# A hybrid encoder on one core: two norms' sums taken through TensorE in reduced-precision halves, and half of a late token tile scaled by GpSimd and VectorE

## The chip, the core and the metric

The program runs on one core of a Trainium2 chip. The core has a matrix engine (TensorE, PE in the profile, whose weight loads are listed apart as PEld), three engines for elementwise work (VectorE or DVE, ScalarE or ACT, GpSimd or POOL), and SyncE (SP), which here only issues transfers. Every engine runs its own queue of instructions in order; they wait for one another through semaphores. Matrix products are accumulated in PSUM, and everything else lies in SBUF. The metric is the device time of one execution in microseconds (us), the median of several runs.

## What is computed

The input is a sequence of 512 tokens with 1024 features, in float32. It passes two layers, each a mixer and an MLP with a residual sum, and a last norm:

```python
for layer in range(DEPTH):                       # DEPTH = 2
    h = rms_norm(x, norm_mix[layer])
    y = stick_breaking_attention(h, ...) if layer % 2 == 0 else rglru_block(h, ...)
    x = x + y
    h = rms_norm(x, norm_mlp[layer])
    x = x + squared_relu_mlp(h, mlp_w1[layer], mlp_w2[layer])
return rms_norm(x, norm_final)

def rms_norm(x, g):
    return x * lax.rsqrt(jnp.mean(x * x, axis=-1, keepdims=True) + EPS) * g
```

The change bears on three of the five norms: the one ahead of the attention, the one ahead of the second mixer (a gated linear recurrence behind a convolution of four taps), and the last one.

## The kernel before

**Layout.** Up to the last MLP the residual stream is held with features on the partitions: 8 tiles `x[c]` of 128 features by 512 tokens. There the mean of squares of a token runs across partitions, and TensorE takes it: a matmul with a 128x128 tile of ones as weights adds up the partitions and leaves the sum on all 128 of them. At the very end tokens are on the partitions: four token tiles `t` of 128 tokens, each in two halves `h` of 512 features, `y(t, h)`. There a norm is a sum along the row.

**Precision.** Almost all products are made in three reduced-precision matmuls (type fp32r): a float32 operand `a` is rounded to a high half (a copy into an fp32r tile, on ScalarE), and the low half is what is left (a subtraction, on VectorE); `high x high`, `high x low` and `low x high` are added up in PSUM. A matmul whose operands are plain float32 is issued by the chip as two pieces, each with a weight load of its own. The two norms of the change are made with such plain float32 matmuls: `ones` and the moving operand are float32 tiles.

**Norm 1** (`inverse`, lines 452 to 484, ahead of the attention). The first products run on the unnormed input, and the inverse root mean square comes later. Eight tiny matmuls put the sum of squares of each token on its partition (`pc`, 128x4); ScalarE takes the root and VectorE the reciprocal `rc`. To have the same numbers along the free axis, VectorE scales the identity by each column of `rc`, four instructions of 128x128 into the tile `diag` (line 473), and TensorE multiplies it by `ones` (line 479): the result `pr` holds the inverse of each token on all partitions. ScalarE copies it to `r` (line 482). The copies `rp` and `rn` with the factors of the scores are made just behind `diag`. These VectorE instructions have high priority for the planner (below). What waits for `r` are the scores' scaling (line 593) and the key halves (line 373).

**Norm 2** (`norm`, `rms`, `inverse` of the second mixer, lines 1580 to 1592). `sq.acc` collects the squares of 8 feature tiles, the last four by VectorE (line 162). In the midst of the product of slab `c2` (a slab is 1024x128 of the input weights) TensorE multiplies `sq.acc` by `ones` (line 1582), ScalarE takes the root (step `N`), VectorE the reciprocal (step `r`).

**The order around it.** TensorE's order is written by hand throughout. In the second mixer ScalarE and VectorE too follow an order written by hand, the string `ORDER`: each step is a letter and a slab, for instance `fz0` fetches the raw weights of slab z0, `az0` rounds them (ScalarE), `xz0` makes their low half (VectorE), `jc3` does so by a transfer that accumulates, `Pz0` multiplies, `n0` scales by `r`, `b0` and `t0` apply the taps, `h0` and `l0` split the result, `G0` multiplies it by the gates' weights. Each instruction of these steps goes behind the one of the step before on its engine (class `Ordered`; its instructions stand under line 789 in the profile). The beginning reads

```python
R0 fz0 fz1 fc3 Pc2 fc4 az0 xz0 az1 N W2 r Pz0 fc5 ac3 jc3 W0 n0 xz1 b0 ac4 t0 fz2 Pz1 W1 jc4 n1 h0 X1
```

Raw weights rotate through three buffers and one more: a fetch on SP's queue waits until the slab that had the buffer has been rounded and subtracted. Elsewhere a planner orders ScalarE, VectorE, GpSimd and SP by a simulation of the program; `tc.issue_after(...)` only holds an instruction behind another of its engine.

**The tail** (`end`, lines 1792 to 1850). The last products of the second MLP arrive one by one and `collect` adds each to `y(t, h)` on VectorE (line 789 in the profile; `mlp.gained` is the last of them). The half h = 0 of the token tiles 2 and 3 comes last, tile 3 in two parts of 256 columns. Helpers: `square` sums the squares of a half (ScalarE, line 1745), `root` takes root (ScalarE, 1764) and reciprocal (VectorE, 1765), `scaled` multiplies a half by the weights `gb` of the last norm (GpSimd, in written order), `one` multiplies a half that is so scaled by the inverse (ScalarE 1787, or VectorE 1789), `both` does both in one instruction (VectorE, 1778), and both of these store the result (SP, 1769). So a half is finished either by `scaled` and `one` or by `both`. `scaled(..., behind=...)` makes GpSimd read a column of another half first, and so wait until that half is done.

Of the kernel before, what the change touches and what calls it, by code (L numbers as in the profile page):

```python
# [11 lines left out]
F32 = mybir.dt.float32  # L12
# [36 lines left out]


ORDER = """
R0 fz0 fz1 fc3 Pc2 fc4 az0 xz0 az1 N W2 r Pz0 fc5 ac3 jc3 W0 n0 xz1 b0 ac4 t0 fz2 Pz1 W1 jc4 n1 h0 X1
ac5 n2 fc6 X0 b2 l0 b1 X2 jc5 G0 t1 az2 Pc3 t2 s0 fz3 h1 ac6 z1 l1 h2 W3 l2 jz2 m0 G1 z0 fc7 n3 G2 s1 X3
R4 Pc4 b3 m1 T0 t3 s2 xc6 E0 E1 fz4 T1 fz6 h3 Pc5 az3 n4 d0 b4 jz3 m2 ac7 t4 E2 T2 jc7 d1 Pz2 n5 q0 d2
h4 az4 l3 W4 k0 fz5 q1 az6 G3 q2 z2 W5 X4 Pc6 b5 k1 fz7 g0 l4 g2 xz4 jz6 t5 g1 fo0 G4 s3 n6 Pz3 y1 h5 y0
# [9 lines left out]
def hybrid_encoder(  # L65
# [41 lines left out]
    def f(ap):  # L107
        return ap.bitcast(F32)
# [7 lines left out]

    dense_ones = work.tile([P, S], BF16, tag="sq", name="dense_ones")
    V.memset(dense_ones[:, :P], 1.0)
    ones = const.tile([P, P], F32, tag="ones", name="ones")
    V.memset(ones, 1.0)  # L120
    ident = const.tile([P, P], F32, tag="ident", name="ident")
    make_identity(nc, ident)
    eps_t = small.tile([P, 16], F32, tag="eps", name="eps_t")[:, :1]
    V.memset(eps_t, EPS)

    xgh = const.tile([P, C, S], F32R, tag="xgh", name="xgh")
# [178 lines left out]
    with ExitStack() as actx:  # L305
# [148 lines left out]
        def inverse():  # L454

            pc = bank("z")
            for t in range(NB):
                PE.matmul(
                    pc[:, t : t + 1], sums[:, t * P : (t + 1) * P], ones[:, 0:1],
                    start=True, stop=True,  # L460
                )
            rc, rp, rn = (small.tile([P, NB], F32, tag=n, name=n) for n in ("rc", "rp", "rn"))
            diag = work.tile([P, S], F32, tag="sq", name="diag")
            with tc.high_priority():
                norm["root"] = A.activation(rc, pc[:, :NB], AF.Sqrt, bias=eps_t, scale=1.0 / D)
                V.reciprocal(rc, rc)
                with tc.issue_after(norm["root"].ins):
                    A.activation(
                        small.tile([P, 1], F32, tag="rt", name="early", bufs=2), eps_t, AF.Sigmoid
                    )  # L470
                for t in range(NB):
                    ts = slice(t * P, (t + 1) * P)
                    V.tensor_scalar(diag[:, ts], ident, rc[:, t : t + 1], None, ALU.mult)
                V.tensor_scalar(rp, rc, SCALE, None, ALU.mult)
                V.tensor_scalar(rn, rc, -SCALE, None, ALU.mult)
            norm.update(rc=rc, rp=rp, rn=rn)
            yield
            pr = bank("z")
            PE.matmul(pr, ones, diag, start=True, stop=True)
            r = work.tile([P, S], F32, tag="r", name="r")  # L480
            with tc.high_priority():
                norm["copy"] = A.copy(r, pr)
            norm["r"] = r
            yield
# [1016 lines left out]
    with ExitStack() as rctx:  # L1501
# [77 lines left out]

        def norm():  # L1580
            ps["norm"] = bank("z")
            PE.matmul(ps["norm"], ones, sq.acc, start=True, stop=True)

        def rms():
            nonlocal r
# [91 lines left out]
        def out_low(c):  # L1677
# [1 line left out]

        STEPS = {  # L1680
            "f": fetch, "a": weights_high, "x": weights_low, "j": weights_added, "P": product,
            "N": rms, "r": inverse, "R": gate_raw, "W": gate_high, "X": gate_low, "G": gates,
            "n": scaled, "b": first_tap, "t": taps, "h": high, "l": low, "s": sigmoids,
            "m": gated_input, "T": tanh, "E": exp, "d": decay, "q": root, "k": recur,
            "z": gate, "g": gelu, "y": times_gate, "u": out_high, "i": out_low,
# [22 lines left out]
    with ExitStack() as mctx:  # L1708
        lp = mctx.enter_context(tc.tile_pool(name="last", bufs=1))
        mlp = Mlp(mctx, 1)  # L1710

        def transposed(h):

            mlp.turns = count(8 * h + 2 * (1 - h))
            for t in range(NB):
                pt = mlp.bank()
                for i in range(4):
                    PE.transpose(
                        pt[:, i * P : (i + 1) * P], x[4 * h + i][:, t * P : (t + 1) * P], ident
                    )  # L1720
                A.copy(mlp.y(t, h), pt)
                mlp.begun.add((t // 2 * 2 + h, t % 2))
            mlp.turns = count(4)

        gb = []
        EG = Ordered(G)

        def factors():
            for h in range(2):
                gb.append(home_tile(*HOMES[h], "gb"))  # L1730
                nc.sync.dma_start(
                    out=gb[h], in_=g_final[:, h * S : (h + 1) * S].broadcast_to([P, S])
                )


        A.activation(lp.tile([P, 1], F32, tag="rt", name="early"), eps_t, AF.Sqrt)

        ss = lp.tile([P, 40], F32, tag="ss", name="ss")[:, : 3 * NB]
        ss = ss.rearrange("p (t i) -> p t i", t=NB)
        bias = lp.tile([P, NB], F32, tag="bias", name="bias")  # L1740

        def square(t, h, i, cols=slice(0, S), end=False):

            junk = work.tile([P, S], F32, tag="sq", name="junk")
            A.activation(
                junk[:, cols], mlp.y(t, h)[:, cols], AF.Square, accum_out=ss[:, t, i : i + 1]
            )
            if not end:
                return A.activation(
                    bias[:, t : t + 1], ss[:, t, i : i + 1], AF.Identity,  # L1750
                    bias=bias[:, t : t + 1] if i else eps_t, scale=1.0 / D,
                )

        def scaled(t, h, cols=slice(0, S), behind=None):

            if behind is not None:
                seen = lp.tile([P, 1], F32, tag="seen", name="seen")
                EG.tensor_copy(seen, behind[:, :1])
            y = mlp.y(t, h)[:, cols]
            EG.tensor_tensor(y, y, gb[h][:, cols], ALU.mult)  # L1760

        def root(t, i):
            rt = small.tile([P, 1], F32, tag="rt", name="rt", bufs=2)
            A.activation(rt, ss[:, t, i : i + 1], AF.Sqrt, bias=bias[:, t : t + 1], scale=1.0 / D)
            V.reciprocal(rt, rt)
            return rt

        def store(t, h, cols=slice(0, S)):
            nc.sync.dma_start(
                out=out[t * P : (t + 1) * P, h * S + cols.start : h * S + cols.stop],  # L1770
                in_=mlp.y(t, h)[:, cols],
            )

        def both(t, h, rt, cols=slice(0, S), last=None):

            y = mlp.y(t, h)[:, cols]
            with tc.issue_after(last.ins) if last else nullcontext():
                done = V.scalar_tensor_tensor(y, y, rt, gb[h][:, cols], ALU.mult, ALU.mult)
            store(t, h, cols)
            return done  # L1780

        def one(t, h, rt, cols=slice(0, S), e=A, last=None):

            y = mlp.y(t, h)[:, cols]
            if e is A:
                with tc.issue_after(last.ins) if last else nullcontext():
                    A.activation(y, y, AF.Copy, scale=rt)
            else:
                V.tensor_scalar(y, y, rt, None, ALU.mult)
            store(t, h, cols)  # L1790

        def end(ws, xs):
            EG.turn(True)
            for t in range(2):
                square(t, 0, 0)
                scaled(t, 0)
                square(t, 1, 1, end=True)
                rt = root(t, 1)
                one(t, 0, rt)
                both(t, 1, rt, last=mlp.gained)  # L1800
            square(2, 1, 0)
            scaled(2, 1)
            square(3, 1, 0)
            scaled(3, 1, behind=mlp.y(1, 1))
            for i in range(2):
                mlp.collect("P4", i, xs[i])
            ps = mlp.bank()
            for g in range(2):
                mlp.times("P4", g, 0, ws[g], ps, True)
            mlp.collect("P4", 0, ps)  # L1810
            square(2, 0, 1, end=True)
            two = root(2, 1)
            parts = [slice(i * HS, (i + 1) * HS) for i in range(2)]
            for i, cols in enumerate(parts):
                ps = mlp.bank()[:, :HS]
                for g in range(2):
                    mlp.times("P4", g, 1, ws[g], ps, True, cols)
                with tc.issue_after(scaled_two.ins) if i else nullcontext():
                    mlp.collect("P4", 1, ps, cols)
                sq = square(3, 0, 1 + i, cols, end=i == 1)  # L1820
                if i == 0:
                    scaled_two = both(2, 0, two)
                    one(2, 1, two, last=sq)
                    scaled(3, 0, cols, behind=mlp.y(2, 0))
            rt = root(3, 2)
            both(3, 0, rt, parts[1])
            one(3, 1, rt)
            one(3, 0, rt, parts[0], V)

        end.ready = factors  # L1830
        mlp.blocks_from_the_third_slab(transposed, end)
# [68 lines left out]
```

## Time and profile before

| | us |
|---|---|
| median of 3 runs | 1026.78 |
| range of the runs | 1025.63 to 1026.83 |
| the profiled execution | 1026.08 |
| its span, from the first to the last instruction | 1024.1 |
| mean granted TensorE clock | 0.998 |

The page of the profile gives for one execution the busy time of each engine, the transfers, the chain of work that ended last (followed back from the last instruction, at each step to what released it) and the costliest groups of instructions. A row of the timeline reads: start in us from the beginning of the span, time in us, engine, line, operation, `out<-in` by the program's names, partitions x elements, and how many instructions are merged; in brackets the idle time of the engine before it and what ended it. A row of the chain reads: start, us, engine, tile and line. A row of waits reads: who waited, for whom, us in total, times, the longest. A row of a group ends with busy us and mean ns of one, then the idle time before. A row of the transfers gives their number, the size of one and the median us from issue to landing. Matmuls overlap one another, so the time of one (0.39 us for 512 columns) is more than the step from one to the next; rows of TensorE name float32 for fp32r operands too. L789 is the line of a helper, so rows there are told apart by their tiles.

### The profile page before, as it was taken

How to read it: one execution, taken by the hardware profiler on the slowest of the kernel's cores; microseconds unless marked ns; L12 is line 12 of the kernel's file. 1: busy time of each engine (PE TensorE's matmuls, PEld its weight loads, DVE VectorE, ACT ScalarE, POOL GpSimd, SP SyncE). 2: the span in 40 equal slices, each digit the busy share in tenths (PEclk: the TensorE clock that was granted, in tenths of full speed). 3: DMA queues.
4: the chain of work that ended last, by engine and by line, in shares of the span. 5: the costliest groups of instructions: out<-in, count | busy, mean ns of one | idle time of the engine just before them, and what ended most of it. 6: DMA issues, size and time to landing. Idle time of an engine off the chain costs nothing.

```text
span 1024.1 us, 16110 instructions
## 1 busy us (share of the span) xinstructions
PE 1015.6 (99%) x5962; PEld 894.1 (87%) x5962; DVE 863.5 (84%) x1152; ACT 708.0 (69%) x1093; POOL 176.3 (17%) x241
## 2 busy tenths in 40 slices
PE   9999999999999999999999999999999999999997
PEld 8988888888888988988988888888988988988986
DVE  7988787847789898898899888986898898898897
ACT  7777676836766863863875799966873763863865
POOL 0454344420010010010011121200010010010013
PEclk9999999999999999999999999999999999999999
DMA  7745454537536667667682575452367567667653
GB/s 239 223 117 146 120 150 102 157 100 285 139 80 198 173 153 200 171 145 201 173 214 81 151 181 162 104 205 83 88 146 202 162 145 203 171 144 203 169 115 108
DMA packets 53550, 161.53 MB, mean 158 GB/s; under 512 B 6752, under 2 KB 8288, under 8 KB 53472
## 3 DMA queue, kind: packets, MB, share of 16 engines
q1 hardware_dynamic: 42240, 120.48, 35.8%
q0 software_dynamic: 10944, 39.85, 22.7%
q8 instruction: 47, 0.77, 0.3%
q14 instruction: 31, 0.25, 0.1%
q10 hardware_dynamic: 288, 0.18, 0.1%
HBM read 138.46 MB, written 4.19 MB: 139 GB/s over the span
## 4 chain that ended last, share of the span: by engine, by line
PE 93%; DVE 3%; ACT 2%; issue 1%; DMA 1%; DVEq 0%; ACTq 0%
PE ps_t L1141 16%; PE ps_acc L1010 9%; PE ps_acc L1141 8%; PE ps_z L1010 8%; PE ps_o L1010 5%; PE ps_acc L234 5%; PE ps_acc L236 5%; PE ps_acc L235 5%; PE ps_z L1141 4%; PE ps_t L234 2%; PE ps_t L235 2%; PE ps_t L236 2%; PE ps_o L234 2%; PE ps_o L236 2%; PE ps_o L235 2%; PE ps_t L628 2%
## 5 line engine op out<-in xcount | busy, mean ns | idle before, releaser
L789 ACT CAST wh<-b 128x1024 fp32r<-128x1024 f32 x174 | 180.5, 1050 | 119.1 <-DVE b L789 77.1
L789 DVE TENSOR_TENSOR wl<-b,wh 128x1024 fp32r<-128x1024 f32 x174 | 210.4, 1219 | 40.3 <-ACT wh L789 38.5
L1086 POOL DMA_DIRECT2D b<-in_w_dn x40 | 34.9, 873 | 292.7 <-DVE b L789 196.4
L234 PE MATMUL ps_acc<-xgh,wh 128*128 128x512 f32 x192 | 78.3, 408 | 0.0
L236 PE MATMUL ps_acc<-xgl,wh 128*128 128x512 f32 x192 | 75.2, 391 | 0.0
L235 PE MATMUL ps_acc<-xgh,wl 128*128 128x512 f32 x192 | 75.1, 391 | 0.0
L1086 POOL DMA_DIRECT2D b<-in_w_up x26 | 22.6, 870 | 297.4 <-DMA b<-in_w_up 81.0
L789 ACT ACTIVATE u<-u 128x512 f32<-128x512 f32 x103 | 65.0, 632 | 12.2 <-DVE u L789 10.4
L606 DVE TENSOR_TENSOR_SCAN scan<-keep,later 128x128 f32<-128x128 f32 (+1 forms) x64 | 58.3, 914 | 17.0 <-ACT keep L596 10.6
L789 DVE TENSOR_TENSOR b<-b,b 128x1024 f32<-128x1024 f32 x50 | 61.2, 1223 | 1.3
L610 POOL TENSOR_TENSOR w<-w,scan 128x128 f32<-128x128 f32 (+1 forms) x64 | 52.7, 825 | 55.3 <-DVE scan L606 50.3
L229 DVE TENSOR_TENSOR wl<-raw,wh 128x512 fp32r<-128x512 f32 (+2 forms) x66 | 56.8, 888 | 5.4 <-ACT wh L227 5.3
L227 ACT CAST wh<-raw 128x512 fp32r<-128x512 f32 (+2 forms) x66 | 46.5, 742 | 21.2 <-PE ps_acc L236 7.3
L789 DVE TENSOR_TENSOR u<-u 128x512 f32<-128x512 f32 (+1 forms) x85 | 54.3, 639 | 4.1 <-ACT u L789 2.3
L789 ACT CAST wh<-raw 128x1024 fp32r<-128x1024 f32 x47 | 49.1, 1047 | 3.4 <-PE ps_acc L1141 3.3
L1010 PE MATMUL ps_z<-xgh,wh 128*128 128x256 f32 x216 | 50.7, 278 | 0.0
L1141 PE MATMUL ps_t<-wh,sl 128*128 128x512 f32 x120 | 46.9, 390 | 0.2 <-DVE sl L789 0.2
L1141 PE MATMUL ps_t<-wh,bl 128*128 128x512 f32 x120 | 46.8, 390 | 0.0
L1141 PE MATMUL ps_t<-wh,bh 128*128 128x512 f32 x120 | 46.8, 390 | 0.0
L1141 PE MATMUL ps_t<-wh,sh 128*128 128x512 f32 x120 | 46.7, 390 | 0.0
L789 DVE TENSOR_TENSOR wl<-raw,wh 128x1024 fp32r<-128x1024 f32 x37 | 45.5, 1229 | 0.8 <-ACT wh L789 0.8
L1010 PE MATMUL ps_acc<-low,wh 128*128 128x256 f32 x192 | 44.7, 276 | 0.0
(419 smaller groups left out, 3210.7 us busy)
## 6 DMA issues: line engine op xcount, KB each, us to landing
b<-in_w_dn SPq DMA_DIRECT2D x48, 512.0 KB, 4.1
b<-in_w_dn POOLq DMA_DIRECT2D x40, 512.0 KB, 5.5
b<-in_w_up SPq DMA_DIRECT2D x39, 512.0 KB, 4.6
b<-in_w_up POOLq DMA_DIRECT2D x26, 512.0 KB, 5.4
raw<-in_w_dn SPq DMA_DIRECT2D x16, 512.0 KB, 4.7
raw<-in_w_in SPq DMA_DIRECT2D x16, 512.0 KB, 4.1
raw<-in_w_up SPq DMA_DIRECT2D x13, 512.0 KB, 3.8
raw<-in_w_qk SPq DMA_DIRECT2D x12, 512.0 KB, 3.9
```

The costliest lines, as they stand in the source:

```text
L227: A.copy(wh[:, k, :], raw[:, k, :])
L229: V.tensor_tensor(wl[:, k, :], raw[:, k, :], f(wh[:, k, :]), ALU.subtract)
L234: PE.matmul(ps, wh, ah, start=start, stop=False)
L235: PE.matmul(ps, wl, ah, start=False, stop=False)
L236: PE.matmul(ps, wh, al, start=False, stop=stop)
L606: V.tensor_tensor_scan(sc[:, S - n : S][:, ::-1], keep[:, :n][:, ::-1], later[:, S - n :][:, ::-1], 1.0, ALU.mult, ALU.max,)
L610: G.tensor_tensor(wt, wt, sc[:, S - n + 1 : S + 1], ALU.mult)
L628: PE.transpose(tr[:, (qb - kb) * P : (qb - kb + 1) * P], w[pair, j, qb][:, kb * P : (kb + 1) * P], ident,)
L789: ins = getattr(self.e, name)(*args, **kwargs)
L1010: PE.matmul(ps[:, i * HS : (i + 1) * HS], m, y, start=new and i == k == low == 0 and y is h, stop=(low, i, k) == steps[-1], skip_group_che ...
L1086: G.dma_start(out=unit[b].rearrange("p j n -> p (j n)"), in_=unit["src"](to), accum_op=ALU.add)
L1141: PE.matmul(sums[to][i], m, y[:, j, :], start=new and g == j == low == 0 and m is h, stop=g == low == j == 1, skip_group_check=not new,)
```

## The change

- `ones` becomes an fp32r tile (`ones_r`), with a float32 view for the other uses.
- Norm 1: VectorE rounds `rc` to a high half (128x4) and subtracts it for the low half, both kept in spare columns of the tile of `eps`; it makes one `diag` of each, eight scalings in place of four, and TensorE adds up two fp32r matmuls.
- Norm 2: two new steps, `H` (ScalarE copies `sq.acc` into an fp32r tile) and `L` (VectorE subtracts it), stand in `ORDER` between `fc3` and `Pc2`; TensorE adds up two fp32r matmuls of the halves.
- Tail: `y(2, 0)` is no longer finished by `both` on VectorE between the two last sums; GpSimd multiplies it by the weights as soon as its squares are summed (`scaled(2, 0)`), and VectorE multiplies it by the inverse behind the last sum (`one(2, 0, two, e=V, last=mlp.gained)`). The last sum is no longer held behind `both(2, 0)`. `scaled(3, 1)` and `scaled(3, 0)` no longer wait for another half (`behind` is left out), and the `seen` copies go with it.

```diff
-R0 fz0 fz1 fc3 Pc2 fc4 az0 xz0 az1 N W2 r Pz0 fc5 ...
+R0 fz0 fz1 fc3 H L Pc2 fc4 az0 xz0 az1 N W2 r Pz0 fc5 ...
...
-    ones = const.tile([P, P], F32, tag="ones", name="ones")
+    ones_r = const.tile([P, P], F32R, tag="ones", name="ones")
+    ones = f(ones_r)
...
-    eps_t = small.tile([P, 16], F32, tag="eps", name="eps_t")[:, :1]
+    spare = small.tile([P, 16], F32, tag="eps", name="eps_t")
+    eps_t = spare[:, :1]
...
-            diag = work.tile([P, S], F32, tag="sq", name="diag")
+            diags = [work.tile([P, S], F32R, tag="sq", name="diag") for _ in range(2)]
+            rch = spare[:, 4:8].bitcast(F32R)
+            rcl = spare[:, 8:12]
...
-                for t in range(NB):
-                    ts = slice(t * P, (t + 1) * P)
-                    V.tensor_scalar(diag[:, ts], ident, rc[:, t : t + 1], None, ALU.mult)
+                V.tensor_copy(rch, rc)
+                V.tensor_tensor(rcl, rc, f(rch), ALU.subtract)
+                for diag, r in zip(diags, (f(rch), rcl)):
+                    for t in range(NB):
+                        ts = slice(t * P, (t + 1) * P)
+                        V.tensor_scalar(diag[:, ts], ident, r[:, t : t + 1], None, ALU.mult)
...
-            PE.matmul(pr, ones, diag, start=True, stop=True)
+            for i, diag in enumerate(diags):
+                PE.matmul(pr, ones_r, diag, start=i == 0, stop=i == 1)
...
-            PE.matmul(ps["norm"], ones, sq.acc, start=True, stop=True)
+            for i, t in enumerate(sums_of_squares):
+                PE.matmul(ps["norm"], ones_r, t, start=i == 0, stop=i == 1)
+
+        sums_of_squares = [work.tile([P, S], F32R, tag="sq", name="ssq") for _ in range(2)]
+
+        def norm_high():
+            OA.copy(sums_of_squares[0], sq.acc)
+
+        def norm_low():
+            OV.tensor_tensor(
+                sums_of_squares[1], sq.acc, f(sums_of_squares[0]), ALU.subtract
+            )
...
-                V.tensor_scalar(y, y, rt, None, ALU.mult)
+                with tc.issue_after(last.ins) if last else nullcontext():
+                    V.tensor_scalar(y, y, rt, None, ALU.mult)
...
-            scaled(3, 1, behind=mlp.y(1, 1))
+            scaled(3, 1)
...
             square(2, 0, 1, end=True)
+            scaled(2, 0)
             two = root(2, 1)
...
-                with tc.issue_after(scaled_two.ins) if i else nullcontext():
-                    mlp.collect("P4", 1, ps, cols)
+                mlp.collect("P4", 1, ps, cols)
                 sq = square(3, 0, 1 + i, cols, end=i == 1)
                 if i == 0:
-                    scaled_two = both(2, 0, two)
                     one(2, 1, two, last=sq)
-                    scaled(3, 0, cols, behind=mlp.y(2, 0))
+                    scaled(3, 0, cols)
+            one(2, 0, two, e=V, last=mlp.gained)
             rt = root(3, 2)
             both(3, 0, rt, parts[1])
             one(3, 1, rt)
```

More of the change, by code (lines that the diff above doesn't have):

```diff
@@ L51 @@
 ORDER = """
-R0 fz0 fz1 fc3 Pc2 fc4 az0 xz0 az1 N W2 r Pz0 fc5 ac3 jc3 W0 n0 xz1 b0 ac4 t0 fz2 Pz1 W1 jc4 n1 h0 X1
+R0 fz0 fz1 fc3 H L Pc2 fc4 az0 xz0 az1 N W2 r Pz0 fc5 ac3 jc3 W0 n0 xz1 b0 ac4 t0 fz2 Pz1 W1 jc4 n1 h0 X1
 ac5 n2 fc6 X0 b2 l0 b1 X2 jc5 G0 t1 az2 Pc3 t2 s0 fz3 h1 ac6 z1 l1 h2 W3 l2 jz2 m0 G1 z0 fc7 n3 G2 s1 X3
@@ L1681, in hybrid_encoder @@
             "f": fetch, "a": weights_high, "x": weights_low, "j": weights_added, "P": product,
-            "N": rms, "r": inverse, "R": gate_raw, "W": gate_high, "X": gate_low, "G": gates,
+            "H": norm_high, "L": norm_low, "N": rms, "r": inverse, "R": gate_raw, "W": gate_high, "X": gate_low, "G": gates,
             "n": scaled, "b": first_tap, "t": taps, "h": high, "l": low, "s": sigmoids,
```

## The prediction

> **What bounds the kernel now.** I read the page first (busy shares, chain), then TensorE's waits, then the chain and the timeline around the three edited places.
>
> ```profile
> span 1024.1 us, 16110 instructions
> ...
> PE 1015.6 (99%) x5962; PEld 894.1 (87%) x5962; DVE 863.5 (84%) x1152; ACT 708.0 (69%) x1093; POOL 176.3 (17%) x241
> ...
> PE 93%; DVE 3%; ACT 2%; issue 1%; DMA 1%; DVEq 0%; ACTq 0%
> ```
>
> TensorE is busy for 99% of the span and the chain that ended last is 93% TensorE. A busy PE proves little by itself, so I asked what it waited for:
>
> ```profile
> PEld ps_z L587 <- ACT keep L596: 0.4, 1, 0.4
> PEld ps_o L655 <- DVE lastl L644: 0.4, 1, 0.4
> ```
>
> These two, both in the attention, are typical: every wait in that view but the one at the very start is 1 us or less in total. So TensorE work that is taken out shortens the run almost one for one, other engines' work costs nothing while it stays ahead of TensorE, and the only long stretch that TensorE does not set lies behind its last matmul.
>
> **The two norm matmuls.** In the chain's pieces each sum that is broadcast through `ones` stands alone:
>
> ```profile
> 25.69 0.86 PE ps_z L479 x2
> ...
> 289.11 2.72 PE ps_t L1141 x12
> ...
> 573.77 0.86 PE ps_z L1582 x2
> ```
>
> A full-precision matmul over 512 columns is issued as two pieces and takes 0.86 us. Reduced-precision (fp32r) matmuls of the same 128x512 shape go at 2.72 / 12 = 0.227 us each. The new code issues two of them for each norm: 2 x 0.227 = 0.45. Gain 0.86 - 0.45 = 0.41 us for each place, 0.82 for both, if TensorE does not have to wait for the new halves.
>
> **Norm 1, the halves of the inverse.** Added on VectorE: a 128x4 copy, a 128x4 subtraction and four more 128x128 scalings, all ahead of the matmul.
>
> ```profile
> 23.13 0.18 DVE L466 RECIPROCAL rc<-rc 128x4 f32<-128x4 f32 x1 [0.24 <-ACT rc L465]
> ...
> 23.43 0.87 DVE L473 TENSOR_SCALAR diag<-ident,rc 128x128 f32<-128x128 f32 x4
> ...
> 25.16 1.29 DVE L209 TENSOR_TENSOR wl<-raw,wh 128x512 fp32r<-128x512 f32 x2 [0.71 <-ACT wh L206]
> ...
> 25.53 1.02 PE L479 MATMUL ps_z<-diag,ones 128*128 128x512 f32 x2
> ...
> 27.69 0.69 DVE L350 TENSOR_TENSOR xl<-ps_t,xh 128x512 fp32r<-128x512 f32 x1 [1.24 <-ACT xh L349]
> ```
>
> Four scalings take 0.87 us, so eight take 1.74; the two small ones, priced like the reciprocal with the gap to its successor (23.43 - 23.13 = 0.30 each at most), add 0.3 to 0.6. From 23.43 the low half is complete at 23.43 + 1.74 + 0.3..0.6 = 25.5 to 25.8. The second matmul can start at 25.53 + 0.23 = 25.76: a stall between nothing and 0.05 us. If writing fp32r from this operation were slower than writing f32 (the trace has no such scaling), say by half, 0.4 us more would stand on the path and the gain of this norm would be gone; I take no stall and keep 0.4 for the range. The 1.2 us by which VectorE falls behind end in the 0.71 us that it idles before the value weights and the 1.24 us before the key halves; without that room it would be a delay of the first scores of the same size.
>
> **Norm 2, the halves of the sum of squares.** The copy H (ScalarE) and the subtraction L (VectorE) stand early in the hand-written order, so on ScalarE the two weight roundings az0 and az1 now queue behind H, which waits for the last sum; the table load and the root (N) queue behind those.
>
> ```profile
> 564.00 1.03 ACT L789 CAST wh<-raw 128x1024 fp32r<-128x1024 f32 x1
> ...
> 567.33 1.28 ACT L789 ACT_TABLE_LOAD   x1
> ...
> 568.62 2.93 DVE L162 TENSOR_TENSOR ssq<-ssq,sq 128x512 f32<-128x512 f32 x4
> ...
> 572.72 20.66 SPq L1549 DMA_DIRECT2D raw<-in_w_in  x5
> ...
> 573.61 1.02 PE L1582 MATMUL ps_z<-ssq,ones 128*128 128x512 f32 x2
> ...
> 574.66 0.69 ACT L789 ACTIVATE r<-ps_z,eps_t 128x512 f32<-128x512 f32 x1 [6.05 <-PE ps_z L1582]
> ...
> 579.45 1.21 DVE L789 TENSOR_TENSOR wl<-raw,wh 128x1024 fp32r<-128x1024 f32 x1
> ...
> 580.26 1.04 ACT L789 CAST wh<-raw 128x1024 fp32r<-128x1024 f32 x1
> ...
> 582.67 0.19 PEld L235 LDWEIGHTS ps_o<-xgh,wl 128*128 128x128 f32 x1
> ...
> 585.38 0.69 DVE L789 TENSOR_TENSOR bl<-bt,bh 128x512 fp32r<-128x512 f32 x1
> ...
> L789 ACT CAST sh<-u 128x512 fp32r<-128x512 f32 x49 | 30.3, 617 | 0.7
> ...
> raw<-in_w_in SPq DMA_DIRECT2D x16, 512.0 KB, 4.1
> ```
>
> The last sum ends at 568.62 + 2.93 = 571.55. H costs 0.62 (the group of 512-wide roundings), L 0.69: the halves are there at 572.86, and TensorE asks at 573.61, so 0.75 us are left and nothing is lost on TensorE. On ScalarE the queue is H, two roundings and the table load: 571.55 + 0.62 + 2 x 1.03 + 1.28 = 575.5, against 574.66 before, so the root comes up to 0.85 us later; the 6.05 us in which ScalarE idled hide the rest. What is late next is VectorE: reciprocal, first scaling, then the low half of slab z1, which ends at 579.45 + 1.21 = 580.66 now and is read at 582.67. 2.0 us of room against 0.85. Past that room TensorE would wait one for one. On SP's queue the fetch that waits for z0's raw buffer goes out at 572.72 now and lands some 4.1 us later, 576.8; the first rounding that may need it runs at 580.26, so 0.85 us more are hidden there too. I price the whole edit at nothing.
>
> **The tail.** It changes the order behind the last matmul.
>
> ```profile
> 1002.11 3.84 POOL L789 TENSOR_TENSOR c<-c,gb 128x512 f32<-128x512 f32 x1 [3.27 <-ACT junk L1745]
> ...
> 1002.45 2.35 DVE L789 TENSOR_TENSOR wl<-b,wh 128x1024 fp32r<-128x1024 f32 x2
> ...
> 1012.69 1.30 POOL L789 TENSOR_TENSOR c<-c,gb 128x512 f32<-128x512 f32 x1 [0.69 <-ACT junk L1745]
> ...
> 1014.01 0.19 ACT L1745 ACTIVATION_READ_ACCUMULATOR junk<-c 128x1 f32 x1
> ...
> 1015.19 0.74 DVE L1778 SCALAR_TENSOR_TENSOR c<-c,rt,gb 128x512 f32<-128x512 f32 x1
> ...
> 1016.13 1.28 POOL L789 TENSOR_TENSOR c<-c,gb 128x512 f32<-128x512 f32 x1
> ...
> 1016.36 0.42 ACT L1745 ACTIVATE junk<-c 128x256 f32<-128x256 f32 x1
> ...
> 1016.59 1.37 DVE L1778 SCALAR_TENSOR_TENSOR c<-c,rt,gb 128x512 f32<-128x512 f32 x1
> ...
> 1016.83 0.28 PE L1104 MATMUL ps_t<-wh,sl 128*128 128x256 f32 x1
> ...
> 1017.10 0.71 ACT L1787 ACTIVATE c<-c,rt 128x512 f32<-128x512 f32 x1
> ...
> 1017.88 0.47 DVE L789 SCALAR_TENSOR_TENSOR c<-ps_t,rr,c 128x256 f32<-128x256 f32 x1
> ...
> 1018.39 0.42 ACT L1745 ACTIVATE junk<-c 128x256 f32<-128x256 f32 x1 [0.58 <-DVE c L789]
> ...
> 1019.86 0.35 DVE L1789 TENSOR_SCALAR c<-c,rt 128x256 f32<-128x256 f32 x1
> ...
> 1019.97 1.31 SPq L1769 DMA_DIRECT2D out<-c  x3
> ```
>
> The last matmul ends at 1016.83 + 0.28 = 1017.11, but the sum that takes it starts only at 1017.88: VectorE is still in `both(2, 0)`, 1.37 us at 1016.59, where the same instruction took 0.74 at 1015.19. The difference is GpSimd's multiplication at 1016.13: both read two tensors of SBUF. The change takes `both(2, 0)` away from there, so the last sum may start 0.77 us earlier. The square behind it, however, also queues on ScalarE behind `one(2, 1)`, which ends at 1017.10 + 0.71 = 1017.81; the square can move from 1018.39 to 1017.81 at best, 0.58 us, and root, last scalings and the three stores at 1019.97 follow it.
>
> What is given back: `scaled(3, 1)` no longer waits for `both(1, 1)`. It becomes ready at 1014.01 + 0.19 = 1014.2 and takes about 1.3 us, to 1015.5 or a little later, across `both(1, 1)` at 1015.19. If GpSimd is first, as at 1016.13, that instruction ends 0.3 to 0.6 us late, the next sum, its square at 1016.36 and `one(2, 1)` with it, and the gain falls from 0.58 to between 0 and 0.3. If VectorE is first, as at 1002.45, where GpSimd's multiplication stretched to 3.84, VectorE loses nothing. I take 0.35. The moved half (`scaled(2, 0)` on GpSimd, then `one(2, 0)` on VectorE) costs nothing if GpSimd is through with two multiplications by about 1018.2: VectorE's part, priced by the 0.35 us of the 256-wide form, at most 0.7, fits while ScalarE squares and takes the root; its store goes out ahead of the last three, so SP's queue gets no longer at the end. If GpSimd is late, VectorE stands there with the last reciprocal behind it.
>
> The Trainium skill, page "SBUF — State Buffer", section "SBUF: two separate sides", says that VectorE and GpSimd share a port pair that whoever starts first keeps for its whole instruction. The pair at 1016.13 and 1016.59 agrees (0.74 became 1.37). By that rule alone the unguarded `scaled(3, 1)` starts first and the tail gains nothing: that is the first rival below.
>
> **Sum.** 0.82 + 0.35 = 1.17 us off the profiled execution, which took 1026.08 (span 1024.1 and 2.0 around it): 1024.9. That execution lies 0.70 below the median of 1026.78 and within its runs, so on the median's scale it is 1026.78 - 1.17 = 1025.6. With both open prices at their bounds (stall 0.4 and tail 0; no stall and tail 0.58) it is 1026.4 to 1025.4.
>
> **Rivals.**
>
> *GpSimd goes first and the tail gains nothing.* For it: 1016.13 against 1016.59. Against it: 1002.45. Then only the norms count, and a late GpSimd may cost up to 0.4: 1026.0 to 1026.4.
>
> *The halves do not do what they say*, because two reduced matmuls with their weight loads and waits take as long as the one they replace. Against it stand the twelve in 2.72 us. 1026.4.
>
> *More than the sum.* The tail gets the whole 0.77, and the instruction order of the attention, which a planner derives anew from shorter and longer instructions, loses the two 0.4 us waits quoted at the top: 0.82 + 0.77 + 0.8 = 2.4, 1024.4.
>
> *Slower: the attention's last weights come late.* Only TensorE's order there is written by hand.
>
> ```profile
> 194.68 3.99 DMA raw<-in_w_so
> ```
>
> This is a piece of the chain: around it the chain does not run through TensorE, so a delay there reaches TensorE undiminished. If the 1.2 us of new high-priority VectorE work at 23 us turns the planned order of the other engines so that one such load goes out one buffer later, the price is up to 3.99: 1025.6 + 4.0 = 1029.6. It decides from a stall of 3.3 us on (1.17 + 2.1); below that it only eats the gain. Against it: the delay is absorbed by about 28 us, and nothing near 190 is edited.
>
> **How the numbers follow.** From no change, about 0.2% (2.1 us) can be told in this kernel: 1024.7 and 1028.8 are the borders. Forecast 0.49 (own range 1025.0 to 1026.4), tail lost 0.11, halves without effect 0.04, more than the sum 0.22, slower 0.14. The first three lie within the borders: same 0.64, faster 0.22, slower 0.14. The range takes in the faster rival and half of what a smaller attention stall would cost: 1024.0 to 1027.9.
>
> **What would show it.** In the changed profile each norm should be two matmuls that take 0.45 us together in the chain, with no wait of TensorE for `diag` or `ssq`; ScalarE's root of norm 2 between 574 and 575.5 and no new TensorE wait before 600; the last sum right behind the last matmul; `both(1, 1)` at 0.74 or stretched to over 1, which tells the tail's two cases apart. The prediction is wrong if TensorE waits for a low half, if its total of waits in the attention moves by over 1 us, or if the last reciprocal is found behind `one(2, 0)`.

## The result, and the profile after

The changed kernel is slower: 1028.42 us, median of 14 runs, against 1026.49 of 14 runs of the kernel before beside them; ratio 1.0021, 95% interval 1.0015 to 1.0028. The prediction was 1025.6 with a range up to 1027.9. The page after:

```profile
span 1026.1 us, 16120 instructions
...
PE 1018.0 (99%) x5962; PEld 896.1 (87%) x5962; DVE 866.1 (84%) x1159; ACT 708.7 (69%) x1094; POOL 177.2 (17%) x240
...
PE 94%; DVE 2%; ACT 2%; issue 1%; POOL 0%; DVEq 0%; ACTq 0%
```

TensorE carries out the same number of matmuls as before, two of them made cheaper at each norm, and is busy for 2.4 us longer (1018.0 against 1015.6). It didn't wait more: it worked longer. So I compared the chains of the two kernels product by product. First the places that were edited, in the chain after (start, us, engine, tile, line; lines were added ahead, so L479 is L487 now and L1582 is L1591):

```profile
25.48 0.45 PE ps_z L487 x2
...
572.96 0.45 PE ps_z L1591 x2
```

Both norms take 0.45 instead of 0.86. At the second the changed kernel is 0.81 us ahead when it starts (573.77 before) and 1.22 when it ends; 0.21 of that lead stands already at the first (25.69 before), ahead of anything that was edited. Then the last MLP, in the chain of the kernel before:

```profile
762.15 5.44 PE ps_t L1141 x24
...
773.03 5.44 PE ps_t L1141 x24
778.47 2.72 PE ps_z L1141 x12
...
786.63 11.05 PE ps_acc L1010 x96
```

and the same products in the chain after:

```profile
760.84 5.52 PE ps_t L1149 x24
...
771.88 5.53 PE ps_t L1149 x24
777.40 2.79 PE ps_z L1149 x12
...
785.72 11.37 PE ps_acc L1018 x96
```

Here it is: 1.31 us ahead at the first row, and every row after it is longer than its twin, with no wait among them. 24 matmuls take 5.52 instead of 5.44, 12 take 2.79 instead of 2.72, and 96 matmuls of the up products (256 columns) take 11.37 instead of 11.05. The clock is not it: the granted one is 1.00 in both kernels in each of the stretches 760 to 850, 850 to 930 and 930 to 1016 us. At the last matmul (1016.83 before) the lead has become a lag:

```profile
1016.58 1.48 POOL L797 TENSOR_TENSOR c<-c,gb 128x512 f32<-128x512 f32 x1 [0.29 <-ACT junk L1764]
...
1017.49 1.12 DVE L1797 SCALAR_TENSOR_TENSOR c<-c,rt,gb 128x512 f32<-128x512 f32 x1
...
1019.14 0.28 PE L1112 MATMUL ps_t<-wh,sl 128*128 128x256 f32 x1
1019.46 0.48 DVE L797 SCALAR_TENSOR_TENSOR c<-ps_t,rr,c 128x256 f32<-128x256 f32 x1 [0.38 <-PE ps_t L1112]
...
1019.78 0.71 ACT L1806 ACTIVATE c<-c,rt 128x512 f32<-128x512 f32 x1
...
1020.39 0.40 ACT L1764 ACTIVATE junk<-c 128x256 f32<-128x256 f32 x1
...
1021.85 0.35 DVE L1809 TENSOR_SCALAR c<-c,rt 128x256 f32<-128x256 f32 x1
...
1021.96 1.33 SPq L1788 DMA_DIRECT2D out<-c  x3
```

These are rows of the timeline of the tail after. The last matmul is 1019.14 - 1016.83 = 2.31 us late, so 1.31 + 2.31 = 3.62 us were lost in the last MLP, in what took 1016.83 - 762.15 = 255 us before. From the last matmul to the three last stores it takes 2.82 now and took 1019.97 - 1016.83 = 3.14: the tail gives 0.32 back. 2.31 - 0.32 = 2.0 is the difference of the two spans.

Which matmuls became slower? In the groups of TensorE from 760 to 1010 us, kept apart by tiles, the second last number is the mean ns of one; before:

```profile
L1141 PE MATMUL ps_t<-wh,bh 128*128 128x512 f32 x56 | 21.8, 390 | 0.0
L1141 PE MATMUL ps_t<-wh,sl 128*128 128x512 f32 x55 | 21.5, 391 | 0.2 <-DVE sl L789 0.2
...
L1141 PE MATMUL ps_t<-wl,sh 128*128 128x512 f32 x52 | 13.9, 389 | 0.0
...
L1010 PE MATMUL ps_o<-s,wh 128*128 128x256 f32 x48 | 11.2, 277 | 0.0
L1010 PE MATMUL ps_o<-low,wh 128*128 128x256 f32 x48 | 11.2, 277 | 0.0
```

and after:

```profile
L1149 PE MATMUL ps_t<-wh,bh 128*128 128x512 f32 x56 | 21.8, 390 | 0.0
L1149 PE MATMUL ps_t<-wh,sl 128*128 128x512 f32 x52 | 20.7, 398 | 0.2 <-DVE sl L797 0.2
...
L1149 PE MATMUL ps_t<-wl,sh 128*128 128x512 f32 x52 | 14.2, 394 | 0.0
...
L1018 PE MATMUL ps_o<-low,wh 128*128 128x256 f32 x48 | 12.0, 288 | 0.0
L1018 PE MATMUL ps_o<-s,wh 128*128 128x256 f32 x48 | 12.0, 284 | 0.0
```

In these names the first operand is the moving one (512 or 256 columns), the second the stationary one, 128x128, whose load is listed under PEld. `bh` is as fast as before; `sh`, `sl` and `s` (the tile `s41`) are slower by 5 to 7 ns each. What the three have in common, and `bh` has not, is that their tiles were moved in SBUF. `scaled(..., behind=...)` made GpSimd copy one column into a tile `seen`. With the last `behind` gone that tile is gone too. It has one column of 4 bytes, takes 32 bytes of each partition, and stood in the pool of the tail, ahead of all tiles of the last MLP. So the tiles of these pools all start 32 bytes lower (bytes from the start of a partition, as the compiled programs place them):

```
          c0       s41      sh       sl       sh modulo 256
before    140544   167168   199936   214272     0
after     140512   167136   199904   214240   224
```

The weight slabs `wh` and `wl` and the tiles `bh`, `bl`, `xgh` and `xgl` did not move. `low` is slower too, 288 instead of 277, and yet only one of its eight tiles was moved (28 of its 224 matmuls read that one). Its matmuls alternate with those of `s`, one by one. So an operand that was moved is not the only one to lose: the matmul beside it does too.

### The profile page after: what moved, and what is told of

It is laid out like the page before. It is cut to its first block, busy times and chain, and to the rows that moved or that the text cites. A ratio compares the mean times of both kernels' runs of the same rounds, so it can differ in the third digit from the quotient of the medians.

```text
span 1026.1 us, 16120 instructions
## 1 busy us (share of the span) xinstructions
PE 1018.0 (99%) x5962; PEld 896.1 (87%) x5962; DVE 866.1 (84%) x1159; ACT 708.7 (69%) x1094; POOL 177.2 (17%) x240
## 4 chain that ended last, share of the span: by engine, by line
PE 94%; DVE 2%; ACT 2%; issue 1%; POOL 0%; DVEq 0%; ACTq 0%
PE ps_t L1149 16%; PE ps_acc L1018 9%; PE ps_acc L1149 8%; PE ps_z L1018 8%; PE ps_acc L236 5%; PE ps_acc L238 5%; PE ps_acc L237 5%; PE ps_o L1018 5%; PE ps_z L1149 4%; PE ps_t L236 2%; PE ps_t L237 2%; PE ps_t L238 2%; PE ps_t L636 2%; PE ps_o L236 2%; PE ps_o L238 2%; PE ps_o L237 2%
```

## The experiments

Two theories. **Place**: the loss comes from where the tiles of the last MLP start; the order of the work has nothing to do with it. **Order**: the planner's new order, or the other instructions of the tail and the norms, slow TensorE. Every ratio below is against the kernel before on the same chip.

**1. The place undone, the place alone, and each half of the change alone.** `ss` is a tile of the same pool that stands ahead of `seen`, with room to spare; its width moves what follows. pad_back is the changed kernel, with

```diff
-        ss = lp.tile([P, 40], F32, tag="ss", name="ss")[:, : 3 * NB]
+        ss = lp.tile([P, 48], F32, tag="ss", name="ss")[:, : 3 * NB]
```

shift_before is the kernel before with 32 columns in place of 40: not one instruction differs, but the last MLP's tiles start 32 bytes lower. norms_alone keeps the old tail (and `seen`); tail_alone keeps the old norms and has `ss` at 48.

> The changed kernel with the tile ss eight floats wider (48 for 40): the 32 bytes that the removed tile seen took in its pool are back, so every tile of the last MLP starts at the address it had before; the order of instructions on all engines is that of the changed kernel. Placement theory (TensorE reads operands that start 32 bytes off a multiple of 64 more slowly; the loss of 3.6 us between 747 and 1014 us is that): the loss goes and norms and tail remain, 1026.5 - 0.9 - 0.3 = about 1025.1 to 1025.3, TensorE's steps in the last MLP back at 0.227 us for 512 columns. Order theory (the planner's new order or the rotated work buffers cost TensorE the time): nothing changes, 1028.4.

> The kernel before with the tile ss eight floats narrower (32 for 40): the tiles of the last MLP start 32 bytes lower, as in the changed kernel, and nothing else differs, not one instruction's place. Placement theory: 1026.5 + 3.6 = about 1030.1, with the loss in the last MLP alone. Order theory: 1026.5, nothing changes.

> The kernel before with the two norms in halves and the tail as before; the last MLP's addresses are those of before. Placement theory: the norms' gain alone, two times 0.41 to 0.45, 1025.6. Order theory with the norms at fault (the work buffers rotate one further): 1028.4 + 0.3 = about 1028.7.

> The kernel before with the changed tail alone, norms as before, ss at 48 so that the addresses are those of before. Placement theory: the tail's gain alone, 0.3, so 1026.2, which cannot be told from no change by the time; in its trace the last reciprocal should stand 0.3 us nearer to the last matmul. Order theory with the tail at fault: 1028.4 + 0.9 = about 1029.3.

| | median | ratio | interval |
|---|---|---|---|
| pad_back | 1025.15 | 0.9984 | 0.9975 to 0.9993 |
| shift_before | 1030.39 | 1.0036 | 1.0023 to 1.0048 |
| norms_alone | 1025.76 | 0.9994 | 0.9985 to 1.0003 |
| tail_alone | 1026.17 | 0.9994 | 0.9986 to 1.0003 |

The chain of pad_back in the last MLP:

```profile
772.48 5.44 PE ps_t L1149 x24
777.92 2.72 PE ps_z L1149 x12
...
786.08 11.05 PE ps_acc L1018 x96
```

and that of shift_before:

```profile
773.18 5.53 PE ps_t L1141 x24
778.71 2.79 PE ps_z L1141 x12
...
787.02 11.37 PE ps_acc L1010 x96
```

Eight columns of padding bring the steps of before back into the changed kernel, and 32 bytes less take them out of the kernel before. Order falls, place holds. norms_alone and tail_alone, in the old places, are not slower either; neither can be told from no change by its time, but in tail_alone the last reciprocal comes 1019.66 - 1017.54 = 2.12 us behind the last matmul instead of 1019.25 - 1016.83 = 2.42, nearer by the 0.3 that was expected. With the place put right the change is what it was meant to be, faster than before by 0.16%.

**2. Which operands pay.** Both kernels have the instructions of the changed one. split_back is pad_back with `s41` 32 bytes wider in the last MLP: what stands behind it (`sh`, `sl` and raw weights that TensorE does not read) is moved by 32 bytes, `s41` and what stands ahead of it are not. split_front is the complement: `ss` at 40 columns as in the changed kernel and the wider `s41`, so that only `sh` and `sl` are back in their old places.

```diff
-            self.s41 = self.bp.tile([P, C // 2, S], F32R, tag="s41", name="s41", bufs=1)
+            s41 = self.bp.tile([P, C // 2 * S + 8 * layer], F32R, tag="s41", name="s41", bufs=1)
+            self.s41 = s41[:, : C // 2 * S].rearrange("p (k s) -> p k s", k=C // 2)
```

> As the one with `ss` at 48 columns, and the last MLP's `s41` 32 bytes wider, so that `sh`, `sl` and the raw slabs behind it stand 32 off while the accumulators, `s41` and the low halves ahead of it stay at multiples of 64. If each operand pays for its own start: 108 matmuls each of wh x sl, wh x sh and wl x sh pay 7.5, 4.8 and 4.4 ns, 1.80 us: 1027.0. If one tile (say the accumulators, read by the other engines) carries the whole loss: 1025.2 or 1028.4.

> The complement: `ss` at 40 columns as in the kernel after, and `s41` 32 bytes wider, so that `sh` and `sl` are back at multiples of 64 while the accumulators, `s41` and the first low halves stay 32 off. If each operand pays for its own start: the rest of the loss, 3.3 - 1.8 = 1.5: 1026.6. If one tile carries all: 1025.2 or 1028.4.

split_back took 1027.2 (ratio 1.0008, 0.9999 to 1.0016), split_front 1026.99 (1.0006, 0.9997 to 1.0015): each between pad_back and the changed kernel. The chain of split_back:

```profile
773.10 5.53 PE ps_t L1149 x24
...
786.95 11.06 PE ps_acc L1018 x96
```

and of split_front:

```profile
772.51 5.44 PE ps_t L1149 x24
...
786.11 11.37 PE ps_acc L1018 x96
```

The loss comes apart: the products with `sh` and `sl` are slow in the one, those with `s41` (and the `low` beside it) in the other. Adding up, matmul by matmul, how much later the next one starts than in pad_back, over the whole last MLP from its first up product on (us):

```
              512 columns   256 columns
before           -0.06         -0.01
after             1.84          1.66
split_back        1.71          0.30
split_front       0.08          1.69
```

So 1.84 + 1.66 = 3.50 us of loss, nearly all of the 3.62, are steps of matmuls whose operands were moved, or that stand among those, half in the down products, where the moved tile is stationary, and half in the up products, where it is moving. The 0.30 of split_back is neither: none of those operands was moved. It is a stretch of slow steps of the kind that part 4 is about.

**3. Which places are good.** The changed kernel with other widths of `ss`.

> As the kernel after with `ss` widened from 40 to 56 columns: the tiles of the last MLP stand 64 bytes higher than in the kernel after, their remainder against 64 bytes stays 32. If the remainder decides: slow again, 1028.2 to 1028.6 (1.0017 times the kernel before). If only the exact old addresses, or simply any address above the kernel after's, are good: at or between 1025.1 and 1026.5.

> As the kernel after with `ss` at 64 columns: 96 bytes higher, remainder 0. If the remainder against 64 bytes decides: 1025.0 to 1025.4, as with 48 columns. If only the exact old addresses are good: 1028.4.

> As the kernel after with `ss` at 80 columns: the tiles of the last MLP stand 128 bytes above where they stood in the kernel before. Moved by 64 bytes they were slow (1030.4). If the position within 128 bytes decides, 128 is as good as 0: 1025.0 to 1025.4. If only the exact old addresses are good, or each byte of distance costs: 1028 to 1031.

> As the kernel after with `ss` at 144 columns: the last MLP's tiles 256 bytes above where they stood in the kernel before. Moves by -32, 32, 64 and 128 bytes were all slow. If the place within 256 bytes decides (the first MLP's `sh`, at 199680, is as fast as the last one's at 199936, 256 bytes apart): 1025.0 to 1025.4, and wh x sh at 389 in the profile's mean. If only the old addresses are good for this MLP: 1028 to 1031.

> As the kernel after with `ss` at 112 columns. The run pad_256, with 144 columns, stood 96 columns or 384 bytes above the fast place of 48 columns, not 256 as its expectation said; 384 is 128 of 256, and its matmuls take the steps of pad_128. With 112 columns the tiles stand 64 columns or 256 bytes above. If the place within 256 bytes decides: 1025.0 to 1025.4, and wh x sh back at 389 in the profile's mean. If only the old addresses are good: 1029 to 1031.

| `ss`, columns | kernel | moved against before, bytes | `sh` modulo 256 | ratio | interval |
|---|---|---|---|---|---|
| 40 | after | -32 | 224 | 1.0021 | 1.0015 to 1.0028 |
| 48 | pad_back | 0 | 0 | 0.9984 | 0.9975 to 0.9993 |
| 56 | pad_more | 32 | 32 | 1.0024 | 1.0015 to 1.0032 |
| 64 | pad_most | 64 | 64 | 1.0038 | 1.0025 to 1.0050 |
| 80 | pad_128 | 128 | 128 | 1.0034 | 1.0022 to 1.0047 |
| 112 | pad_256_true | 256 | 0 | 0.9986 | 0.9977 to 0.9995 |
| 144 | pad_256 | 384 | 128 | 1.0035 | 1.0021 to 1.0048 |

My first reading, that a start must be a multiple of 64 bytes, was wrong: pad_most is a multiple of 64 and slower than the changed kernel. The run called pad_256 moved the tiles by 384 bytes and not by the 256 that its expectation names; it agrees with pad_128, with which it shares the place modulo 256, and pad_256_true made up for the slip. In its chain

```profile
777.97 2.72 PE ps_z L1149 x12
780.69 5.44 PE ps_t L1149 x24
786.13 11.05 PE ps_acc L1018 x96
```

every step is back. As far as these moves show (0 and 256 are alike, and 128 and 384), the place within 256 bytes decides; of the five places tried, 0 is the good one for these tiles.

**4. What the good place depends on.** The up products' weight slabs start 64 bytes behind a multiple of 256 (`UP_AT = 16` columns), those of the first product of each quarter 144 bytes behind (`OPEN_AT = 36`). All four kernels here are pad_back with one of these numbers changed: up_at_0 has `UP_AT` 0; open_at_48, open_at_32 and open_at_16 have that `OPEN_AT`.

```diff
-    ROOM, UP_AT, V_AT = 64, 16, 48
+    ROOM, UP_AT, V_AT = 64, 0, 48
...
-        OPEN_AT = 36
+        OPEN_AT = 48
```

> As the one with `ss` at 48 columns, but the weight slabs of all up products of both MLPs begin at their tile's start instead of 64 bytes behind it, so that stationary and moving operand of the 256-wide matmuls both stand at 0 of 128. If what counts is how the stationary operand stands to the moving one within 128 bytes, and 256-wide matmuls want 64 between them: some 2100 of them go from 113.4 to 118 or more, 9.7 us, about 1034.8. If each operand counts by itself and 0 of 128 is the good place: 1025.2 or a little less.

> As the one with `ss` at 48 columns, but the first up product of each quarter has its weights 192 bytes (64 of 128) behind the slab's start instead of 144 (16 of 128). If a stationary operand 64 of 128 off the moving one is the good place: the 144 matmuls that take 119.5 now go to 113.4, 0.88 us: 1024.3. If the odd start sets the rhythm of the products behind it, and an even one leaves them in the slow rhythm of 118 that the start of the last MLP shows: up to 1700 x 4.4 = 7.5 us more, at most 1032.

> The same with 128 bytes (0 of 128). If the period is 64 bytes: as with 192 bytes. If it is 128 and the 256-wide matmuls want 64 between their operands: the 144 stay at 118 to 120, 1025.2, and later products may keep the slow rhythm.

> As the one with `ss` at 48 columns, with the first up product of each quarter at 64 bytes like the other up products. If 64 bytes between the operands by itself makes the fast step: 144 matmuls go from 119.5 to 113.4, 1024.3. If the rhythm that the products before have left goes on until something breaks it: they stay at 118 and products behind them may too, 1025.0 to 1029.

up_at_0 took 1036.03 (1.0096, 1.0081 to 1.0112), open_at_48 1024.81 (0.9985, 0.9976 to 0.9993), open_at_32 1025.36 (0.9988, 0.9980 to 0.9997), open_at_16 1031.44 (1.0049, 1.0037 to 1.0062). A row of the up products of the first MLP in the chain of pad_back:

```profile
340.50 2.72 PE ps_z L1018 x24
```

of up_at_0:

```profile
340.71 2.88 PE ps_z L1018 x24
```

and of open_at_16:

```profile
340.88 2.83 PE ps_z L1018 x24
```

Two things follow. With both operands at 0 modulo 256 a matmul of 256 columns takes 2.88 / 24 = 120 ns instead of 113, while one of 512 columns has its fast step just there (5.44 / 24 = 227): the good place of the stationary operand is not the same in the two kinds of product, so a tile has no good place of its own. And in open_at_16 the operands of this row stand where they stand in pad_back; only the weights of the first product of the quarter, 24 matmuls that begin 120 ahead of this row, were moved, to the very place that is good for the others. Still all up products behind it in the quarter go at 2.83 / 24 = 118, and the time is beyond the 1029 that was given for this case. A slow rhythm, once there, persists through products that would be fast otherwise. The odd 144 bytes of `OPEN_AT` give those 24 matmuls a step of 120, but leave the ones behind them in the fast rhythm, and so do 192 and 128 bytes. open_at_48 gained less than the 0.88 us expected, since its own 24 went only to 118; it can't be told from pad_back by its time, and either beats both kernels of the change.

A start is not the only thing that brings the slow rhythm. In split_back not one tile of the first MLP stands elsewhere than in pad_back, and its chain there reads

```profile
354.00 2.72 PE ps_o L1018 x24
...
356.73 3.09 PE ps_z L1018 x24
359.82 2.83 PE ps_o L1018 x24
```

At 356.73 a weight load waited 0.20 us for ScalarE; from there to the end of the quarter's up products the step is 118 instead of 113, and the next quarter is fast again. In the last MLP a pause at 810 us of pad_back (two steps of 144 and 225 ns) is followed by steps of 118, and the next one at 816 us (185 and 223) by 113 again; in open_at_32 the steps stay at 118 behind the second one (187 and 226). The up products that begin at 728 us have no slab at `OPEN_AT`, and there the kernel before too goes at 2.83 for 24 matmuls. So place is not all that decides the rhythm, and 0.3 us between two runs can come from such a stretch alone; what a wait does to it is seen here and not explained.

**5. The guard brought back.** tail_guard is the changed kernel with `scaled(3, 1, behind=mlp.y(1, 1))` again, and so with `seen`.

> As the kernel after, but `scaled(3, 1)` waits for `both(1, 1)` again; the tile `seen` that this wait needs is back with it, so the last MLP's tiles stand where they stood in the kernel before. `both(1, 1)` back at 0.74 instead of 1.12; if the unguarded multiplication costs what the prediction said (0.23 of the 0.58): 1024.9 against 1025.15 for the padded one; if the later multiplications of GpSimd take that back: 1025.2 to 1025.6. If placement were not the cause of the loss, 1028.

It took 1025.58 (0.9992, 0.9983 to 1.0001), without padding: one more witness for the place. Its tail:

```profile
1014.55 0.74 DVE L1797 SCALAR_TENSOR_TENSOR c<-c,rt,gb 128x512 f32<-128x512 f32 x1
...
1016.51 0.48 DVE L797 SCALAR_TENSOR_TENSOR c<-ps_t,rr,c 128x256 f32<-128x256 f32 x1 [0.59 <-PE ps_t L1112]
1017.93 0.17 DVE L1784 RECIPROCAL rt<-rt 128x1 f32<-128x1 f32 x1 [0.94 <-ACT rt L1783]
1018.04 0.93 DVE L1809 TENSOR_SCALAR c<-c,rt 128x512 f32<-128x512 f32 x1
...
1019.28 0.34 DVE L1809 TENSOR_SCALAR c<-c,rt 128x256 f32<-128x256 f32 x1
```

`both(1, 1)` is back at 0.74, and the last reciprocal comes 1.42 us behind the start of the last sum, 0.37 sooner than in the changed kernel (1021.25 - 1019.46 = 1.79). But GpSimd's three multiplications run later (3.19 us from 1015.50 on), so `one(2, 0)` (1018.04) now stands between the last reciprocal and the last scalings, and the last scaling starts 1019.28 - 1016.51 = 2.77 behind that sum, against 1021.85 - 1019.46 = 2.39. By these rows the unguarded multiplication is the better one, by 0.38 us; the times cannot tell (0.9992 here, 0.9984 in pad_back, with intervals that overlap).

## Why the prediction was wrong, step by step

**The norms: right.** Predicted 0.45 for each pair, measured 0.45. The rows of norm 1 and 2 after:

```profile
23.43 1.65 DVE L480 TENSOR_SCALAR diag<-ident,eps_t 128x128 fp32r<-128x128 f32 x8
...
25.32 0.62 PE L487 MATMUL ps_z<-diag,ones 128*128 128x512 f32 x2
```

```profile
571.00 0.69 DVE L797 TENSOR_TENSOR ssq<-ssq 128x512 fp32r<-128x512 f32 x1 [0.74 <-ACT ssq L797]
...
574.18 0.69 ACT L797 ACTIVATE r<-ps_z,eps_t 128x512 f32<-128x512 f32 x1
```

Eight scalings end at 25.08, ahead of the matmul; writing fp32r costs nothing extra (1.65 / 8 = 0.21 against 0.87 / 4 = 0.22), so the 0.4 kept for that was not needed. (It was also too small for its own condition: all eight scalings write fp32r, and half of 1.74 is 0.87.) At norm 2 the low half is there at 571.69 and TensorE asks at 572.96. The root starts at 574.18, within the 574 to 575.5 that were given, and no new wait of TensorE follows. norms_alone, 0.6 us faster by its ratio with an interval that includes none, does not contradict 0.82.

**The tail: right in size, in part by luck.** 0.35 predicted, 0.32 measured. But 0.35 was a choice between 0.58, if VectorE goes first, and 0 to 0.3, if GpSimd does. GpSimd did go first (1016.58 against 1017.49) and stretched `both(1, 1)` from 0.74 to 1.12. The Trainium skill's rule of the shared port pair (page "SBUF — State Buffer", section "SBUF: two separate sides") is right about the direction; by its full block VectorE would have lost all the 0.57 us until GpSimd's 1016.58 + 1.48 = 1018.06, and it lost 0.38, which decides here (times of GpSimd are rough). The first rival's price did not follow: the last sum still starts right behind the last matmul, and the square behind it waits only for `one(2, 1)`. The moved half takes 0.87 us, priced at 0.7 at most, and still ends ahead of the last reciprocal, as assumed. One reading was loose: at 1002.45 GpSimd, at work since 1002.11, is the earlier of the two rows shown. What makes VectorE the first there is the instruction before, which is not among them: `sl`, 0.68 us from 1001.85 on.

**The attention: right that nothing happens there.** The rival that puts 4 us on a late weight load did not occur; the changed kernel is ahead through all of it.

**What failed** is the sentence that opens the part on the tail: "It changes the order behind the last matmul." It priced the removed waits as order alone. They also free a tile, the tile stood ahead of others, and 32 bytes of place cost TensorE 3.6 us in work that no line of the diff touches. The sum held that term at nothing without naming it, and took the step of a matmul, 0.227 us, as fixed. None of the rivals had it: the slower one was put into the attention because there the chain leaves TensorE, while the real loss lay where the chain is mostly TensorE, in the length of its steps. The first part already had the number that should have led there: TensorE is busy for 99% of the span, so a change of 0.4% in its step is 4 us, more than all terms of the sum. The sum itself, -1.17, agrees with pad_back, the change without the move: 0.9984 of 1026.5 is -1.6, with an interval from -2.6 to -0.7.

## What to carry to other kernels

In a kernel that TensorE bounds, removing or adding a tile, even one of 4 bytes a partition, can move all that is allocated behind it: compare where the operands of the matmuls start before and after, and keep the places (here modulo 256 bytes) with a few columns of padding. When a change loses time in code that it does not touch, compare the chain product by product; equal counts with longer rows and no waits are the sign of slower steps, and the groups kept apart by tiles name the operands (and at times the neighbour of one, as `low` here). Measure an edit with the places held fixed, or its own worth can't be read: here a gain of 0.16% was seen as a loss of 0.21%.

## What the runs showed of the hardware

The step of an fp32r matmul depends on where its operands start: 227 ns at 512 columns in pad_back and about 234 with `sl` in the changed kernel, 113 at 256 columns in pad_back and 120 in up_at_0. As far as moves of 256 and 384 bytes show, the pattern repeats after 256 bytes. The stationary operand counts although its load is a row of its own under PEld and overlaps the matmul before: in split_back only stationary operands of the 512-wide products were moved, and they lost 1.58 us (with the other 512-wide ones 1.71). The Trainium skill, page "SBUF — State Buffer", section "A bandwidth-pool intuition that's wrong (but worth ruling out)", gives TensorE a second, independent read port for weight loads. The runs do not show whether its two reads collide on anything, but they show that the place of the one changes the step.

The second surprise is that the step has a memory: a product of the same instructions with the same operands in the same places ran at 113 or at 118 ns per matmul, according to where the first product of its quarter had its weights (pad_back and open_at_16), or from a wait of 0.2 us on (split_back). It would also explain how products of tiles that were not moved got slower in pad_most, where the group of `xgl` and `wh` took a mean of 281 ns instead of 276 in pad_back:

```profile
L1018 PE MATMUL ps_z<-xgl,wh 128*128 128x256 f32 x72 | 17.4, 281 | 0.0
```

Open is why: whether it is the difference of the two starts or each by itself together with the width, and why one wait starts or ends a slow rhythm and another does not. No run here separates these.
